# Small loads of the gated delta net issued from GpSimd's queue

## The chip, the cores and the metric

The kernel runs on one core of one Trainium2 chip. The metric is device time in microseconds (us), the median over several executions. Each engine (TensorE or PE, VectorE or DVE, ScalarE or ACT, GpSimd or POOL, SyncE or SP) runs its own instructions in order and waits for the others by semaphores. A DMA is issued by an instruction in the queue of one engine, here SP, ACT or POOL, and an issuing instruction that must wait holds back what stands behind it in that queue. The data then moves on 16 DMA engines that all queues share.

## The reference

A decoder of two layers on 272 tokens (16 learned ones in front of 256) and 2048 channels, in float32. Layer 0 mixes tokens with a short gated convolution, layer 1 with a gated delta net; a gated feed-forward follows each.

```python
def chunked_gated_delta_rule(q, k, v, g, beta):
    ...                                    # chunks of tokens, decay from cumulated g
    t_mat = inverse of (I + strictly lower part of (beta k k^T * decay))
    u_c = t_mat @ (v * beta);  w_c = t_mat @ (k * beta * exp(g))
    for each chunk:                        # the state S goes from chunk to chunk
        v_new = u_i - w_i @ S
        o_i = q_g @ S + (q k^T * decay) @ v_new
        S = S * g_last + k_tail^T @ v_new

def gated_deltanet_mixer(h, ...):          # 16 key heads, 32 value heads of width 128
    qkv, z, b, a = split(h @ w_in)
    ...
    o = rmsnorm(chunked_gated_delta_rule(...), norm_w) * silu(z)
    return o @ w_out
```

## The kernel before

All large products stream their weights. A piece of weights (128 x 1024 float32, 512 KB) is loaded into one of a few `raw` buffers by SP (L95), split exactly into two parts, `whi` by ACT (L108) and `wlo` by DVE or sometimes POOL (L109), and multiplied three times per block by PE (L265 to L267). SP may load a piece only when the split of an earlier one has freed its buffer.

The program order of every engine is fixed: it is the order in which Python emits the instructions (`in_program_order`). `Clockwork` deals this order out in ticks, about one for every 12 large matmuls. `ck.later(n, f)` emits `f` n ticks later, and `ck.side` runs a generator a bit in each tick.

In layer 1 the kernel first computes gates, keys, queries and output gates z. Keys, queries and z go to DRAM (`Kd`, `Qd`, `Zd`), as do the decays `Dd`, the inverses of the diagonal blocks `Ud` (of each 92-token chunk), the blocks `Md`, `Vd` and the factors `Ed`, `Ekd`. Then, between the products with the value weights and the output weights, `cores` runs 16 pairs of value heads. `pair` works as follows.

- It first emits 16 loads, all in one tick: `kh`, `qh` (128 x 276), two each of `D` and `U` (92 x 276, in rows of 92), of `U2`, `M2`, `V2` (46 x 138, in rows of 46) and of the two `e` tiles (128 x 276, one row broadcast to all partitions). `load` (L881) is the helper for D, U, U2, M2 and V2; L894 loads the `e` tiles. The profile names U2, M2, V2 as U, M, V.
- Seven ticks later (`LW`) comes the preparation, in two steps: transposes of kh (L900), products of M2 and U2 (L905), POOL's products of the `e` tiles (L911), products with V2 (L917), POOL's product of U (L922).
- When fewer than two pairs are in their recurrence, the pair starts its own, three chunks of three steps, a step every two ticks. The next pair's loads are emitted one tick after that.
- Two ticks after a pair's last step, `tail` norms its output, `scale` lets POOL multiply (`ot`, L1001) and, right behind that in program order, loads two z tiles (`zl`, L1005). Three ticks later `back` lets DVE form `y` (L1018) from the z tile, and ACT and DVE split it.

The buffers: D, U and kt have three, the `e` tag six (three pairs), kh, qh and zl two, U2, M2 and V2 one.

Of the kernel before, what the change touches and what calls it, by code (L numbers as in the profile page):

```python
# [15 lines left out]
P = 128  # L16
# [5 lines left out]
class Dims:  # L22
# [23 lines left out]
    def gdn_order(self):  # L46
        """the units of the gated delta net: gates, keys, output gates, queries, values, output products"""
        seq = [("ba", 0)] + [("k", j) for j in range(self.NK)] + [("q", j) for j in range(self.NK)]
        seq += [("z", j) for j in range(self.ZE)]
        v = [("v", j) for j in range(self.NV)]  # L50
        z = [("z", j) for j in range(self.ZE, self.NV)]
        for s in range(self.NST):
            seq += v[:self.VA[s]]
            v = v[self.VA[s]:]
            n = len(z) if s == self.NST - 1 else 0
            seq += z[:n]
            z = z[n:]
            seq += [("o", s * self.KT + j) for j in range(self.KT)]
        return seq


class Stream:
    """Weights: DMA, exact split into two float32r parts, some pieces ahead of the products."""

# [11 lines left out]
    def widen(self, pool, raw_bufs, part_bufs):  # L76
        """more buffers for the pieces a0 .. a1 - 1"""
        self.xpool, self.XR, self.XP = pool, raw_bufs, part_bufs
# [48 lines left out]
class Clockwork:  # L127
    """Program order: what runs beside the products is put between their pieces."""

# [46 lines left out]
def trunk(ctx: ExitStack, tc: tile.TileContext, d: Dims, xT, par, w_s0, w_sc, w_sco, w_q, w_k, w_v, w_z, w_ba,  # L176
# [10 lines left out]

# [1 line left out]
    cp = ctx.enter_context(tc.tile_pool(name="const", bufs=1))  # L189
# [17 lines left out]

# [1 line left out]
    def pieces(nk):  # L209
# [25 lines left out]

    # the first products go block by block of channels, as these arrive
    for g in range(KT // G4):
# [42 lines left out]

# [1 line left out]
    hq = [cp.tile([P, G4, T], F32, name=f"h{g}") for g in range(KT // G4)]  # L282
# [15 lines left out]
    def rsqrt_steps(pool, out, v, np_, w, ty, tt, bufs=1):  # L298
        """out = v ** -0.5 : estimate from the exponent, then three Newton steps."""
        y = pool.tile([np_, w], F32, tag=ty, name="rsy", bufs=bufs)  # L300
        t = pool.tile([np_, w], F32, tag=tt, name="rst", bufs=bufs)
        nc.vector.tensor_scalar(out=t.bitcast(I32), in0=v.bitcast(I32), scalar1=1, scalar2=None,
                                op0=ALU.logical_shift_right)
        nc.vector.tensor_scalar(out=y.bitcast(I32), in0=t.bitcast(I32), scalar1=-1, scalar2=0x5F3759DF,
                                op0=ALU.mult, op1=ALU.add)
        for it in range(3):
            nc.vector.tensor_tensor(out=t, in0=y, in1=y, op=ALU.mult)
            nc.vector.scalar_tensor_tensor(out=t, in0=v, scalar=-0.5, in1=t, op0=ALU.mult, op1=ALU.mult)
            nc.vector.scalar_tensor_tensor(out=(out if it == 2 else y), in0=t, scalar=1.5, in1=y,
                                           op0=ALU.add, op1=ALU.mult)  # L310
            yield

    class Norm:
        """x = h * w, split; the per-token factor Rt joins where products leave PSUM."""

# [31 lines left out]
        def finish_last(self):  # L347
            """a token in each partition, then back to a token in each column"""
            a, nt = self.a, (T - self.a) // P
            ps = psum(nt)  # L350
            for i in range(nt):
                for s in (self.acc, self.sq):
                    nc.tensor.matmul(ps[:, i:i + 1], s[:, a + i * P:a + (i + 1) * P], ones[:, 0:1],
                                     start=s is self.acc, stop=s is self.sq)
            v = tp.tile([P, nt], F32, tag="lv", name="lv", bufs=1)
            nc.vector.tensor_scalar(out=v, in0=ps, scalar1=1.0 / d.D, scalar2=EPS, op0=ALU.mult, op1=ALU.add)
            r = tp.tile([P, nt], F32, tag="lr", name="lr", bufs=1)
            for _ in rsqrt_steps(tp, r, v, P, nt, "ly", "lt"):
                pass
            pt = psum(nt * P)  # L360
            for i in range(nt):
                nc.tensor.transpose(pt[:, i * P:(i + 1) * P], r[:, i:i + 1].to_broadcast([P, P]), ident)
            nc.scalar.copy(out=Rt[:, a:T], in_=pt)
# [24 lines left out]

# [1 line left out]
    pctx = more_psum()  # L390
# [31 lines left out]
    with tc.tile_pool(name="scy", bufs=1) as yp, tc.tile_pool(name="sct", bufs=2) as sp:  # L422
# [47 lines left out]
        def resid(nrm, ps, j, a, mode, lag=0):  # L470
            """h += product; what the next norm needs of it, lag units later"""
            nc.vector.tensor_tensor(out=h[j][:, a:T], in0=ps, in1=h[j][:, a:T], op=ALU.add)  # L472
# [30 lines left out]

# [1 line left out]
    def ffn(seq, a, nxt, last):  # L505
# [35 lines left out]

# [1 line left out]
    # a value head 2 j + e of the reference has the row e NK + j here  # L543
    def dram(name, shape):
# [26 lines left out]
    def conv_in(ps, pool, ci, a=0):  # L571
        """causal convolution of width 4 of a unit of the projection, from token a"""
        x1 = pool.tile([P, T], F32, tag="cx", name="cx")
# [17 lines left out]
    st.widen(pha.enter_context(tc.tile_pool(name="wx", bufs=1)), d.XR, d.XP)  # L591
    # a matrix and room to step from its first to its second diagonal block
    W2 = 2 * (H * C + H)
# [73 lines left out]

    # keys, queries
    onehot = ka.tile([P, 2 * NK - 1], F32, name="onehot")
# [15 lines left out]

    # outputs are asked for from token M0 on: queries before it stay zero
    QA = M0 - 4
# [34 lines left out]
    def q_norm(qs):  # L722
        """1 / length of the queries of each token, a column for each chunk of a head"""
        v = small("qv", NK, T)
# [17 lines left out]
    def k_norm(Wt):  # L742
        """1 / length of the keys from the diagonals of their products"""
        for _ in range(d.IL):
# [60 lines left out]
    def inverse(Wt, ri):  # L805
        """unit triangular matrices, one in each partition: the inverses of both diagonal blocks. The heads' own
        preparation joins them to the inverse of the whole; Md takes the block between them, Vd the first inverse,
        both transposed"""
        flat = Wt[:, :CC]
# [50 lines left out]

    # values, recurrence, output
    vts = {}
# [5 lines left out]
    def pair(j, vp):  # L868
        """two heads that share their keys"""
        kh = vp.tile([P, TP], F32, tag="kh", name="kh")  # L870
        nc.sync.dma_start(out=kh, in_=Kd[j])
        qh = vp.tile([P, TP], F32, tag="qh", name="qh")
        nc.sync.dma_start(out=qh, in_=Qd[j])
        JN = slice(j * N, (j + 1) * N)

        def load(tag, src, a, b, bufs, r=slice(None), c=slice(None)):
            """a block of a matrix of each chunk of both heads"""
            t = vp.tile([a, 2, N, b], F32, tag=tag, name=tag, bufs=bufs)
            for e in range(2):
                g = e * NK + j  # L880
                nc.sync.dma_start(out=t[:, e], in_=src[g * N:(g + 1) * N].rearrange(  # L881
                    "n (s c) -> s n c", c=(C if src.shape[1] == CC else H))[r, :, c])
# [7 lines left out]
        for x, xd in ((qg, Ed), (kg, Ekd)):  # L890
            t = vp.tile([P, 2, TP], F32, tag="e", name="e", bufs=6)
            for e in range(2):
                g = e * NK + j
                nc.sync.dma_start(out=t[:, e], in_=xd[g:g + 1, :].broadcast_to([P, TP]))  # L894
            x.append(t)
# [91 lines left out]
        def tail():  # L987
            """norm over the value channels, gate"""
            v = ov.rearrange("c e n -> c (e n)")
# [7 lines left out]
        def scale(steps, ro):  # L997
# [5 lines left out]
            for e in range(2):  # L1003
                z.append(vp.tile([P, S], F32, tag="zl", name="zl", bufs=2))
                nc.sync.dma_start(out=z[e], in_=Zd[2 * j + e])  # L1005
            ck.later(3, lambda: back(0))
# [18 lines left out]
    def cores(vp):  # L1025
        """the recurrences: one pair of heads loads and prepares while others run, a step at a time"""
        wait, core, nxt, started = [], [], 0, 0
# [89 lines left out]

# [1 line left out]
    for k in range(KT):  # L1119
# [9 lines left out]
def in_program_order(tc):  # L1129
    """each engine runs its instructions in the order in which they stand above"""  # L1130
    last = {}
# [9 lines left out]
def layout(d, x, meta_tokens, mixer_norm, ffn_norm, sc_w_in, sc_conv_w, sc_w_out, gdn_w_in, gdn_conv_w, gdn_a_log,  # L1141
# [12 lines left out]

    # the products with the first two groups of columns: block of channels, pair of products, row, ...
    first = np.stack([units(sc_w_in[0][:, g * D:g * D + 2 * P]) for g in range(3)], axis=1)
# [59 lines left out]
```

## Time and profile before

| | |
|---|---|
| time, median of 3 runs | 3058.52 us (3055.4 to 3060.13) |
| profiled execution, first to last instruction (span) | 3051.3 us |
| PE busy | 2910.4 us (95%) |
| DVE, ACT, POOL busy | 61%, 42%, 15% |
| DMA bytes | 539.52 MB, 177 GB/s on average |

The times of the runs lie 4 to 9 us above the span of the profiled execution, which holds only what lies between the first and the last instruction. Busy shares are means over all stages. The pairs of heads run between about 1682 and 2202 us.

### The profile page before, as it was taken

To read this page: it belongs to the slowest core of one execution; us is meant where nothing else is said; L and a number is where in the kernel's file an instruction comes from. 1 tells how busy PE (TensorE), PEld (TensorE's weight loads), DVE (VectorE), ACT (ScalarE), POOL (GpSimd) and SP (SyncE) were. 2 spreads that over 40 slices of the span, in tenths; PEclk is the share of its full clock that TensorE was granted. 3 is DMA by queue.
4 is the path that set the end of the run, shared out by engine and by line. 5 is a ranking of instruction groups with operands and counts; after the bars stand their busy time and mean duration, and the time that the engine had idled before them with its cause. 6 is when DMAs were issued, how large, how long until landed. Compare 5 with 4: busy or idle time off the path is not lost. (4 is left out here: it accounts for less than half of the span.)

```text
span 3051.3 us, 57493 instructions
## 1 busy us (share of the span) xinstructions
PE 2910.4 (95%) x23501; PEld 2875.3 (94%) x23501; DVE 1855.7 (61%) x2570; ACT 1292.7 (42%) x1874; POOL 468.8 (15%) x532
## 2 busy tenths in 40 slices
PE   9999999999999999899988788989899999999998
PEld 8999999999999999888888788888899999999997
DVE  6555555555555456868896466656575555555555
ACT  5334444434334344644333343444354443444434
POOL 2000100000000001524342123322220000000001
PEclk9999999999999999999999889999999999999999
DMA  6555555555555565597556544444555556556565
GB/s 200 191 176 171 178 173 175 176 167 184 178 164 183 168 175 175 166 265 209 184 176 202 155 145 150 147 147 150 160 170 183 184 187 178 196 177 196 184 177 152
DMA packets 212695, 539.52 MB, mean 177 GB/s; under 512 B 55664, under 2 KB 82624, under 8 KB 211952
## 3 DMA queue, kind: packets, MB, share of 16 engines
q1 hardware_dynamic: 208144, 517.92, 54.1%
q0 software_dynamic: 2480, 15.01, 1.7%
q8 instruction: 184, 3.01, 0.4%
q10 hardware_dynamic: 1808, 2.92, 0.3%
q14 instruction: 79, 0.65, 0.1%
HBM read 515.03 MB, written 20.74 MB: 176 GB/s over the span
## 5 line engine op out<-in xcount | busy, mean ns | idle before, releaser
L109 DVE TENSOR_TENSOR wlo<-raw,whi 128x1024 fp32r<-128x1024 f32 (+3 forms) x945 | 1126.0, 1201 | 756.5 <-ACT whi L108 747.7
L267 PE MATMUL mm<-xh,wlo 128*128 128x272 f32 (+2 forms) x5136 | 1479.4, 288 | 34.4 <-POOL wlo L109 22.1
L265 PE MATMUL mm<-xh,whi 128*128 128x272 f32 (+2 forms) x5136 | 1486.7, 289 | 11.9 <-ACT whi L108 11.9
L266 PE MATMUL mm<-xl,whi 128*128 128x272 f32 (+2 forms) x5136 | 1477.0, 288 | 0.5 <-DVE xl L331 0.5
L108 ACT CAST whi<-raw 128x1024 fp32r<-128x1024 f32 (+2 forms) x995 | 962.5, 975 | 542.6 <-PE mm L266 347.1
L267 PEld LDWEIGHTS mm<-xh,wlo 128*128 128x128 f32 x5136 | 978.8, 191 | 41.0 <-POOL wlo L109 26.3
L265 PEld LDWEIGHTS mm<-xh,whi 128*128 128x128 f32 x5136 | 980.1, 191 | 20.6 <-ACT whi L108 12.3
L266 PEld LDWEIGHTS mm<-xl,whi 128*128 128x128 f32 x5136 | 978.0, 190 | 1.2 <-DVE xl L331 1.0
L267 PE MATMUL mm<-ah,wlo 128*128 128x272 f32 (+1 forms) x1408 | 399.3, 284 | 0.0
L265 PE MATMUL mm<-ah,whi 128*128 128x272 f32 (+1 forms) x1408 | 398.9, 283 | 0.0
L266 PE MATMUL mm<-al,whi 128*128 128x272 f32 (+1 forms) x1408 | 398.7, 283 | 0.0
L265 PEld LDWEIGHTS mm<-ah,whi 128*128 128x128 f32 x1408 | 264.9, 188 | 0.0
L267 PEld LDWEIGHTS mm<-ah,wlo 128*128 128x128 f32 x1408 | 264.6, 188 | 0.0
L266 PEld LDWEIGHTS mm<-al,whi 128*128 128x128 f32 x1408 | 264.4, 188 | 0.0
L513 POOL TENSOR_TENSOR u<-u,g 128x272 f32<-128x272 f32 (+1 forms) x88 | 66.5, 755 | 1225.7 <-DVE u L512 1225.7
L580 DVE SCALAR_TENSOR_TENSOR cc<-cx,prm,cc 128x271 f32<-128x271 f32 (+5 forms) x192 | 146.6, 764 | 38.3 <-ACT cc L576 33.3
L109 POOL TENSOR_TENSOR wlo<-raw,whi 128x1024 fp32r<-128x1024 f32 x50 | 131.4, 2627 | 202.1 <-ACT whi L108 163.3
L385 ACT CAST ah<-u 128x272 fp32r<-128x272 f32 (+1 forms) x88 | 36.4, 413 | 289.6 <-POOL u L513 289.6
L343 POOL TENSOR_TENSOR nacc<-nacc,nsq 128x272 f32<-128x272 f32 (+1 forms) x70 | 63.5, 908 | 621.5 <-ACT nsq L341 620.3
L265 PE MATMUL mm<-yh,whi 128*128 128x256 f32 x512 | 152.4, 298 | 0.4 <-DVE h L472 0.4
L266 PE MATMUL mm<-yl,whi 128*128 128x256 f32 x512 | 146.5, 286 | 0.0
L267 PE MATMUL mm<-yh,wlo 128*128 128x256 f32 x512 | 146.4, 286 | 0.0
(327 smaller groups left out, 2316.1 us busy)
## 6 DMA issues: line engine op xcount, KB each, us to landing
raw<-w_gu SPq DMA_DIRECT2D x352, 512.0 KB
raw<-w_dn SPq DMA_DIRECT2D x128, 384.0 KB
raw<-w_sc SPq DMA_DIRECT2D x84, 512.0 KB
raw<-w_dn SPq DMA_DIRECT2D x128, 320.0 KB
raw<-w_z SPq DMA_DIRECT2D x64, 512.0 KB
raw<-w_v SPq DMA_DIRECT2D x64, 512.0 KB
raw<-w_go SPq DMA_DIRECT2D x64, 512.0 KB
raw<-w_sco SPq DMA_DIRECT2D x32, 512.0 KB
```

The source lines that it names most:

```text
L108: self.nc.scalar.copy(out=hi[:, s], in_=t[:, s])
L109: eng.tensor_tensor(out=lo[:, s], in0=t[:, s], in1=hi[:, s].bitcast(F32), op=ALU.subtract)
L265: nc.tensor.matmul(ps, wh, x[0][:, a:b], start=start, stop=False)
L266: nc.tensor.matmul(ps, wh, x[1][:, a:b], start=False, stop=False)
L267: nc.tensor.matmul(ps, wl, x[0][:, a:b], start=False, stop=stop)
L343: nc.gpsimd.tensor_tensor(out=self.acc[:, a:T], in0=self.acc[:, a:T], in1=self.sq[:, a:T], op=ALU.add)
L385: nc.scalar.copy(out=hi, in_=x)
L513: nc.gpsimd.tensor_tensor(out=u1, in0=u1, in1=g1, op=ALU.mult)
L580: nc.vector.scalar_tensor_tensor(out=cv[:, a + i:T], in0=x1[:, a:T - i], scalar=pcol("gcc", 4 * ci + 3 - i), in1=cv[:, a + i:T], op0=ALU.m ...
```

## The change

The DMA instructions of the 16 loads of each pair and of its two z tiles are issued from GpSimd's queue. Each stands in POOL's program order at the place where it stood in SP's. Nothing else is moved; the diff also drops docstrings and comments, which are left out here.

```diff
     def pair(j, vp):
         kh = vp.tile([P, TP], F32, tag="kh", name="kh")
-        nc.sync.dma_start(out=kh, in_=Kd[j])
+        nc.gpsimd.dma_start(out=kh, in_=Kd[j])
         qh = vp.tile([P, TP], F32, tag="qh", name="qh")
-        nc.sync.dma_start(out=qh, in_=Qd[j])
+        nc.gpsimd.dma_start(out=qh, in_=Qd[j])
...
             for e in range(2):
                 g = e * NK + j
-                nc.sync.dma_start(out=t[:, e], in_=src[g * N:(g + 1) * N].rearrange(
+                nc.gpsimd.dma_start(out=t[:, e], in_=src[g * N:(g + 1) * N].rearrange(
...
-                nc.sync.dma_start(out=t[:, e], in_=xd[g:g + 1, :].broadcast_to([P, TP]))
+                nc.gpsimd.dma_start(out=t[:, e], in_=xd[g:g + 1, :].broadcast_to([P, TP]))
...
                 z.append(vp.tile([P, S], F32, tag="zl", name="zl", bufs=2))
-                nc.sync.dma_start(out=z[e], in_=Zd[2 * j + e])
+                nc.gpsimd.dma_start(out=z[e], in_=Zd[2 * j + e])
```

## Rows read from the trace of the kernel before

**Rows 1.** The page: busy time and share of the span, each engine.

```profile
PE 2910.4 (95%) x23501; PEld 2875.3 (94%) x23501; DVE 1855.7 (61%) x2570; ACT 1292.7 (42%) x1874; POOL 468.8 (15%) x532
```

**Rows 2.** Busy time by stretch: length, engines, granted PE clock, DMA share, GB/s.

```profile
1681.60:2201.80 520.20, 454.13 (x3652) 439.15 (x3651) 313.96 (x642) 209.23 (x427) 141.22 (x197) 0.90 0.49 150
1851.00:1863.80 12.80, 12.80 (x111) 12.63 (x110) 7.88 (x23) 4.63 (x9) 3.17 (x3) 1.00 0.38 104
1865.20:1871.70 6.50, 0.92 (x5) 0.29 (x3) 2.00 (x6) 1.21 (x4) 0.00 (x0) 0.82 1.03 303
2300.00:2400.00 100.00, 100.00 (x843) 100.00 (x843) 54.67 (x64) 43.42 (x54) 6.65 (x9) 1.00 0.60 194
```

**Rows 3.** Waits, 1680 to 2250 us: us in total, times, longest.

```profile
POOL sq L980 <- ACT ot L977: 189.7, 26, 14.4
...
ACT whi L108 <- DMA raw<-w_v: 46.2, 8, 13.0
...
DVE y L1018 <- DMA zl<-Zd: 35.7, 7, 9.2
...
PE psd L917 <- ACT Y L908: 32.7, 6, 6.8
...
PE psd L905 <- ACT vn L951: 11.3, 7, 2.0
```

**Rows 4.** SP's queue through one pair's loads: start, length, line, DMA, count.

```profile
1849.73 0.36 SPq L871 DMA_DIRECT2D kh<-Kd  x1
...
1851.74 6.11 SPq L881 DMA_DIRECT2D U<-Ud  x4
1857.89 2.04 SPq L881 DMA_DIRECT2D M<-Md  x2
...
1862.85 0.90 SPq L894 DMA_DIRECT2D e<-Ekd  x2
1863.79 0.91 SPq L1005 DMA_DIRECT2D zl<-Zd  x2
1864.80 14.36 SPq L95 DMA_DIRECT2D raw<-w_v  x5
```

**Rows 5.** Chain of work that ended last: start, length, what.

```profile
1835.32 4.02 DMA zl<-Zd
...
1846.24 0.65 PE psd L917 x12
...
1863.79 4.88 DMA zl<-Zd
...
2036.00 5.78 DMA raw<-w_go
...
2043.77 1.19 PE psd L917 x12
```

**Rows 6.** POOL in order of time: start, length, operation, idle before and releaser.

```profile
1822.73 1.25 POOL L922 TENSOR_TENSOR U<-U,btok 92x276 f32<-92x276 f32 x2 [5.17 <-ACT U L919]
...
1847.89 2.49 POOL L922 TENSOR_TENSOR U<-U,btok 92x276 f32<-92x276 f32 x2
...
2024.30 1.81 POOL L1001 TENSOR_TENSOR ot<-ot,ro 92x384 f32<-92x384 f32 x2 [3.28 <-DVE ro L309]
...
2037.91 1.37 POOL L911 TENSOR_TENSOR e<-e,qh 128x552 f32<-128x552 f32 x1 [2.65 <-PE psd L905]
```

**Rows 7.** Groups of POOL's DMA issues, 1200 to 1690 us: busy us, mean ns.

```profile
L772 POOL DMA_DIRECT2D Wt<-KKd x8 | 4.0, 512 | 6.5 <-DMA KKd<-kk 6.5
...
L759 POOL DMA_DIRECT2D re<-rkd x2 | 1.0, 505 | 0.0
L647 POOL DMA_DIRECT2D glb<-Ld x1 | 0.6, 581 | 0.0
```

**Rows 8.** POOL's DMAs by line: count, KB each, median us from issue to landing.

```profile
glb<-Ld POOLq DMA_DIRECT2D x1, 48.0 KB, 5.1
...
rq<-rqd POOLq DMA_DIRECT2D x1, 17.2 KB, 4.2
```

## The prediction

> **What bounds the kernel now.** The page's first part says PE: busy 95% of the span [rows 1]. That is a mean, so I looked at the stretch in which pairs of heads run, by the view of busy time by stretch [rows 2]. From 1681.6 to 2201.8 us PE is busy 454.1 of 520.2 us at a granted clock of 0.90; from 2300 to 2400 us, where only weights stream, it is busy all the time at 1.00. So 66 us of idle time, and a lower clock around it, are all that this change can win back.
>
> The waits of that stretch [rows 3] show two kinds of stall. In the first, ACT waits for a late piece of weights (46.2 us, 8 times, w_v alone); behind that split in ACT's order stands the copy of `Y`, and PE waits for it before L917: 32.7 us in 6 times. In the second, DVE waits for a z tile before it forms `y` (35.7 us, 7 times); ACT's split of y holds back `vn`, and PE waits at L905 (11.3 us, 7 times) and in what follows. One such stall lies between 1865.2 and 1871.7: PE is busy 0.92 of 6.5 us, at clock 0.82 [rows 2].
>
> What makes both late is SP's queue [rows 4]. The 16 loads of a pair go out from 1849.73 to 1863.75 us, 14.0 us, and no weights in between. The z tiles stand behind them, the weights behind those. Bytes don't set these 14 us: a load of `M` has 24.8 KB and takes 1.02 us, one of `Ekd` 138 KB and takes 0.45. Short rows do: the U loads (rows of 92 and 46 elements) take 6.11 us for four. While they go out, the DMA engines are 38% busy and move 104 GB/s, against 60% and 194 with weights alone [rows 2].
>
> **The change part by part.** It takes 256 loads and 32 z loads out of SP's queue, 14.9 us for each pair, and puts as many instructions on POOL. I treat SP, POOL and the two kinds of stall in turn.
>
> *What 16 loads cost on POOL.* The trace has POOL issues of tiles of 16 rows (`re`), 505 ns, of 48 rows (`Wt`), 512 ns, eight back to back, and of 128 rows (`glb`), 581 ns [rows 7]. None has three runs in a partition. The line through the first and the last is 0.68 ns per run. kh, qh and four e loads have 128 runs (581 ns), four loads of D and U 276 (682), six of U2, M2 and V2 138 (588): 3.5 + 2.7 + 3.5 = 9.7 us. From below: 16 x 0.505 = 8.1 us. From above: what the same 16 cost on SP, 14.0 us, if the thing that paces them there paces POOL. I take 9.7, as it comes from POOL's own rows, and keep both ends. POOL has room: 141 of 520 us busy [rows 2]; 16 x 11 us more makes 61%.
>
> *The stall on the z tile, 7 times.* In these pairs POOL's order is: product of U, the 16 loads, `ot`, the two z loads. By buffers the loads needn't wait: U2, M2 and V2 of the pair before have been read by L905 and L917, which come before the product of U. Before the change, from the end of that product to the landing of the first z tile: 1847.89 + 2.49 = 1850.4 to 1863.79 + 4.88 = 1868.7, 18.3 us; in the shortest pair 1824.0 to 1839.3, 15.4 us [rows 5, 6]. Middle 16.9. After: 9.7 for the loads, 1.8 for `ot` [rows 6], 0.6 for the issue, 5.1 to land, as `glb` needs [rows 8]: 17.2 us. The long path through SP is replaced by one as long through POOL, where `ot`, which SP didn't wait for, is now part of it. 7 x 0.3 = +2 us. Low end 8.1 + 1.8 + 0.5 + 4.2 (`rq`) [rows 8] = 14.6: -16 us. High end 14.0 + 1.8 + 0.6 + 5.1 = 21.5: +32 us.
>
> *The stall on late weights, 6 times.* SP now has nothing ahead of a piece but the wait for its buffer, so it is issued up to 14 us earlier and the 32.7 us go. With them goes some time at the low clock: right after such a stall the twelve L917 take 1.19 us, at full clock 0.65 [rows 5]; with what follows them I count 1 us each time. Together 6 x 6.45 = 39 us. But what is late next is on POOL. In the first two pairs nothing stands ahead of the loads there, and I keep all: 13 us. In the other four, such as the one whose weights land at 2036.00 + 5.78, the loads stand behind `ot`, which waits for DVE until 2024.30 [rows 6]. They start at 2026.1 + 1.2 for the z loads = 2027.3. M2, the ninth and tenth, goes out by 2033.3 and lands at 2038.4, while L905 had finished by 2037.9, when it released POOL's `e` product: 1 us late. The e tiles land at 2027.3 + 9.7 + 5.1 = 2042.1, 4 us late for that product; the product of U stands behind it in POOL's order, and PE needs that for the pair's first step, so I let about half of this come back to PE. I keep 3.3 of 6.45 us, four times: 13 us. Sum -26 us, with ends 0 and -39.
>
> *What queues behind the loads on POOL.* `sq` of the other pair and the e products do; DVE's sum of `sq` waits for it. In the z pairs DVE waits for the z tile later than that anyway; where no stall follows I count nothing, as POOL sits idle 7.3 us on average before `sq` (189.7 us, 26 times) [rows 3] and DVE is busy 314 of 520 us [rows 2]. Without that lead of DVE it costs 9.7 - 7.3 = 2.4 us a pair, at the high end 6.7.
>
> *Rules of the Trainium skill.* The rows say that SP's issue time follows the short rows and not the bytes, with the DMA engines 38% busy [rows 2, 4]. "DMA: Bandwidth & Descriptors" (section "Why a DMA increments its semaphore by 16 and not by 1") says a DMA runs on the largest number of engines, up to 16, that divides the slowest dimension: 4 for 92 partitions, 2 for 46; from SP these are always the lowest-numbered, from GpSimd a cursor moves on from load to load. By that the loads would run beside each other after the change; no run here shows it yet. The same page (section "SWDGE vs HWDGE vs iDMA") speaks against the change: issuing from several engines saves only the issue time, which is usually small beside the transfer. By that nothing would be won; the trace disagrees, as 14.0 us of issue stand against 4.9 us of landing [rows 4, 5].
>
> Sum: +2 - 26 = -24 us. The profiled execution has 3051.3 us of span, the median is 7.2 us above it; -24 makes 3027 of the one and 3034 of the other.
>
> **Rivals.** *POOL is as slow as SP, or slower.* For: the runs of three rows in a partition are on no POOL row, and the U loads cost SP 1.5 us each. Against: POOL's issue hardly grows from 16 to 128 rows. Place: the z pairs, where loads, `ot` and z loads are in a row on POOL. It decides from 26 / 7 = 3.7 us more than before in each of them, that is 13.1 us for 16 loads, 0.82 us each. At 14.0 us, with nothing kept of the late weights since M2 and e land too late, it gives 3058.5 + 32 = 3090; beyond that more.
>
> *The gain is given back.* The weights come early, but in the four later pairs M2, V2 and e come as late as the weights did, and only the first two pairs win, 13 us, while the z pairs lose 7 x 1 to 2 us: 3052 to 3059. For: in the pair at 2027 the e tiles are 4 us late by the sum above. Against: PE doesn't wait for e directly.
>
> *The loads run beside each other.* If what paces them on SP is that few DMA engines serve all of them, and POOL spreads them, they land as fast as POOL issues: the low end in the z pairs and the whole of the weights' term, -16 - 39 = -55, 3003. The first rule of the Trainium skill above is this rival. For: 38% busy engines. Against: the wait of `ot` for DVE and the two-sided price remain.
>
> **How the numbers follow.** Forecast 0.42, spread loads 0.15, given back 0.13, slow POOL 0.30. A measurement of this kernel can tell about 0.2%, 6 us. So faster 0.57, same 0.13, slower 0.30. The time is the forecast's, 3034; its own range is 3015 to 3050. The range of all reaches from the low ends, 3003, to the slow POOL at SP's price, 3090.
>
> **What would show it.** Mean POOL issue of D and U loads 0.6 to 0.7 us: right; over 1.2: wrong, and the sum with it. ACT's wait for w_v and w_go should nearly vanish, and PE's wait at L917 fall below 15 us. DVE's wait for zl should stay near 36 us. If it doubles, POOL is the new bound; if it goes, the loads land faster than I think. PE's granted clock in the stretch should rise from 0.90 to some 0.93.

## The result

The changed kernel takes 3090.31 us (median of 4 runs, 3086.36 to 3092.19), the kernel before on the same chip 3057.57. The ratio is 1.0111, with a 95% interval of 1.0099 to 1.0123: 1.1% slower. The forecast was 3034 us and faster; the time lies 0.3 us past the upper end of the range, at the price of the slow-POOL rival. The profiled execution has 3089.8 us of span, 38.5 more than before. One of the four runs of x12 below took 3963 us at a granted clock of 0.65 and is left out of its row; it is also the run that was traced, so x12 is read by its times alone.

### The profile page after: what moved, and what is told of

It is laid out like the page before. It is cut to its first block, busy times and chain, and to the rows that moved or that the text cites. A ratio compares the mean times of both kernels' runs of the same rounds, so it can differ in the third digit from the quotient of the medians.

```text
span 3089.8 us, 57485 instructions
## 1 busy us (share of the span) xinstructions
PE 2919.9 (95%) x23501; PEld 2881.0 (93%) x23501; DVE 1861.5 (60%) x2570; ACT 1294.6 (42%) x1874; POOL 735.1 (24%) x820
## 5 line engine op out<-in xcount | busy, mean ns | idle before, releaser
L265 PE MATMUL mm<-xh,whi 128*128 128x272 f32 (+2 forms) x5136 | 1489.4, 290 | 10.6 <-ACT whi L108 10.6
L580 DVE SCALAR_TENSOR_TENSOR cc<-cx,prm,cc 128x271 f32<-128x271 f32 (+5 forms) x192 | 144.8, 754 | 37.7 <-ACT cc L576 32.7
```

Source lines behind the costliest of these rows:

```text
L265: nc.tensor.matmul(ps, wh, x[0][:, a:b], start=start, stop=False)
L580: nc.vector.scalar_tensor_tensor(out=cv[:, a + i:T], in0=x1[:, a:T - i], scalar=pcol("gcc", 4 * ci + 3 - i), in1=cv[:, a + i:T], op0=ALU.m ...
```

## The profile after

The page's first part; beside [rows 1], POOL has 288 instructions more and is busy 266 us more, 0.92 us for each.

```profile
PE 2919.9 (95%) x23501; PEld 2881.0 (93%) x23501; DVE 1861.5 (60%) x2570; ACT 1294.6 (42%) x1874; POOL 735.1 (24%) x820
```

Busy time by stretch (columns as in [rows 2]): first the stretch of the pairs with its borders, in the kernel after; then the time in which one pair's 16 loads are issued.

```profile
1640.00:2300.00 660.00, 560.30 (x4433) 541.36 (x4434) 384.88 (x755) 255.16 (x487) 420.39 (x501) 0.90 0.57 148
1864.10:1879.80 15.70, 9.11 (x77) 8.81 (x75) 6.26 (x21) 5.35 (x11) 15.69 (x17) 0.92 0.73 158
```

The same stretch in the kernel before:

```profile
1640.00:2300.00 660.00, 586.75 (x4727) 570.67 (x4726) 411.06 (x811) 276.44 (x530) 167.47 (x226) 0.92 0.50 154
```

PE's idle time in it grows from 73.3 to 99.7 us, by 26.4, and the clock falls from 0.92 to 0.90. PE does 294 matmuls fewer. In the 300 us after it, where weights stream in both kernels, the changed one does 2526; at that rate the 294 are 35 of the 38.5 us. So the loss lies here.

Waits, 1660 to 2300 us, of the kernel after (us in total, times, longest), against [rows 3] (1680 to 2250 us):

```profile
DVE ov L981 <- POOL vt L1105: 67.5, 7, 12.3
DVE ov L981 <- POOL sq L980: 67.3, 12, 12.2
...
PE psc L1016 <- POOL ot L1001: 49.0, 8, 7.5
...
PE psd L905 <- DMA M<-Md: 22.4, 7, 6.6
...
ACT whi L108 <- DMA raw<-w_v: 10.8, 7, 4.2
...
PE psd L905 <- ACT vn L951: 6.5, 2, 5.6
...
PE psd L917 <- ACT Y L908: 4.4, 3, 2.0
...
DVE y L1018 <- DMA zl<-Zd: 3.0, 2, 1.6
```

Both kinds of stall of before are nearly gone: L917 waits 4.4 us and not 32.7, ACT for w_v 10.8 and not 46.2, DVE for the z tile 3.0 and not 35.7. Three others have come in their place. PE waits 49.0 us for `ot` before it transposes it (L1016, in `back`), 22.4 us for M at L905, and DVE 135 us for `sq` or for a small memset that stands behind `sq` in POOL's order (6.2 us before).

POOL in order of time, through one pair's loads, in the kernel after (start, length, what):

```profile
1861.71 2.49 POOL L922 TENSOR_TENSOR U<-U,btok 92x276 f32<-92x276 f32 x2
1864.15 0.59 POOL L871 DMA_DIRECT2D kh<-Kd  x1
1864.73 0.54 POOL L873 DMA_DIRECT2D qh<-Qd  x1
1865.26 2.56 POOL L881 DMA_DIRECT2D D<-Dd  x2
1867.81 4.94 POOL L881 DMA_DIRECT2D U<-Ud  x4
1872.74 2.44 POOL L881 DMA_DIRECT2D M<-Md  x2
1875.17 2.44 POOL L881 DMA_DIRECT2D V<-Vd  x2
1877.60 1.13 POOL L894 DMA_DIRECT2D e<-Ed  x2
1878.72 1.06 POOL L894 DMA_DIRECT2D e<-Ekd  x2
1879.80 1.63 POOL L1001 TENSOR_TENSOR ot<-ot,ro 92x384 f32<-92x384 f32 x2
1881.37 1.12 POOL L1005 DMA_DIRECT2D zl<-Zd  x2
1882.51 0.62 POOL L980 TENSOR_TENSOR sq<-ot 92x256 f32<-92x256 f32 x1
```

The 16 loads take 15.7 us (1864.15 to 1879.80) with no wait among them. `ot`, the z loads and `sq` stand behind them. The two engines that want these, PE and DVE, of the same kernel (in brackets the idle time before and its releaser):

```profile
1880.69 0.72 PE L1016 MATMUL psc<-ident,ot 92*128 92x92 f32 x3 [7.48 <-POOL ot L1001]
```

```profile
1883.16 0.42 DVE L981 TENSOR_REDUCE ov<-sq 92x2 f32<-92x256 f32 x1 [12.22 <-POOL sq L980]
...
1885.30 0.47 DVE L1018 SCALAR_TENSOR_TENSOR y<-psc,prm,zl 128x256 f32<-128x256 f32 x1
```

PE is idle 7.48 us for `ot`, DVE 12.22 us for `sq`. When DVE comes to `y`, the z tile is there.

POOL's groups, 1660 to 2300 us, of the kernel after (count | busy us, mean ns | idle before):

```profile
L881 POOL DMA_DIRECT2D U<-Ud x64 | 78.9, 1238 | 0.0
L881 POOL DMA_DIRECT2D D<-Dd x32 | 41.0, 1284 | 0.0
...
L881 POOL DMA_DIRECT2D M<-Md x32 | 39.0, 1222 | 0.0
...
L1005 POOL DMA_DIRECT2D zl<-Zd x32 | 17.9, 565 | 0.4 <-DMA M<-Md 0.4
...
L871 POOL DMA_DIRECT2D kh<-Kd x16 | 9.3, 582 | 4.2 <-DMA Vd<-wk 4.2
```

The loads of 128 partitions cost what [rows 7] say, 0.54 to 0.58 us. Those of 92 and 46 partitions cost 1.22 to 1.28 us, twice that, whether they have 276 runs (D) or 138 (M).

## The experiments

All ratios are to the kernel before on the same chip; its median was 3051.98 us beside the first four, 3054.09 beside x5 to x8, 3054.98 beside x9 to x12. In kernels with padded rows, line numbers stand 4 to 6 higher.

| kernel | loads on POOL | us | ratio, 95% interval |
|---|---|---|---|
| x2 rows padded | all | 3012.15 | 0.9879 (0.9859 to 0.9900) |
| x3 rows padded | none | 2987.51 | 0.9793 (0.9774 to 0.9811) |
| x4 | all but the ten short-row ones | 3008.83 | 0.9860 (0.9846 to 0.9875) |
| x5 `sq`, `ot` off POOL | all | 3047.48 | 0.9980 (0.9970 to 0.9990) |
| x6 `sq`, `ot` off POOL | none | 3049.03 | 0.9985 (0.9975 to 0.9994) |
| x7 loads two ticks later | all | 3101.82 | 1.0154 (1.0137 to 1.0171) |
| x8 rows padded | all but the ten | 2979.76 | 0.9757 (0.9742 to 0.9772) |
| x9 | z tiles alone | 3037.42 | 0.9941 (0.9922 to 0.9959) |
| x10 padded, `sq`, `ot` off POOL | all | 2983.07 | 0.9762 (0.9748 to 0.9777) |
| x11 padded, `sq`, `ot` off POOL | all but the ten | 2960.57 | 0.9689 (0.9674 to 0.9703) |
| x12 rows padded | z tiles alone | 2989.24 | 0.9789 (0.9771 to 0.9807) |

**What a load costs POOL (x1).** The kernel before, with four loads of each of eight forms from POOL, and as many from SP, behind the last feed-forward. Each form names its partitions, the runs in each and the elements of a run.

```diff
     ffn(seq1, M0, 4, True)
 
+    with tc.tile_pool(name="probe", bufs=1) as pb:
...
+        forms = (("fa", 92, 3, 92), ("fb", 96, 3, 92), ("fc", 92, 1, 276), ("fd", 46, 3, 46), ("fe", 48, 3, 46),
+                 ("ff", 46, 1, 138), ("fg", 128, 3, 92), ("fh", 128, 1, 276))
+        for eng, x in ((nc.gpsimd, "p"), (nc.sync, "s")):
+            for nm_, a, n, c in forms:
...
+                    eng.dma_start(out=t, in_=src)
```

> The kernel before, with eight forms of loads appended after the last feed-forward, four of each back to back, first from POOL, then from SP: fa 92 partitions x 3 runs of 92, fb 96 x 3 x 92, fc 92 x 1 x 276, fd 46 x 3 x 46, fe 48 x 3 x 46, ff 46 x 1 x 138, fg 128 x 3 x 92, fh 128 x 1 x 276. What the POOL issue costs is in dispute; in the changed kernel D, U, M and V cost 1.22 to 1.28 us there, kh, qh and e 0.53 to 0.59. Theory A, the number of partitions (no multiple of 16): fa, fc, fd, ff cost about 1.2 us on POOL, fb, fe, fg, fh 0.5 to 0.6. Theory B, three runs in a partition: fa, fb, fd, fe, fg cost 1.2, fc, ff, fh 0.5 to 0.6. Theory C, the count of runs, which the prediction used: fa and fb 0.7, fd and fe 0.6, fg 0.75. On SP, theory A has fa at 1.3 and fd at 1.0 us once several are queued, and fb, fe, fg near fh's 0.4.

POOL in order of time, in that kernel; the second letter behind "pf" is the one of four, the first the form (a is "fa" above):

```profile
3035.07 1.27 POOL L1127 DMA_DIRECT2D pfab<-w_q  x1
...
3040.15 0.67 POOL L1127 DMA_DIRECT2D pfbc<-w_q  x1
...
3043.93 0.52 POOL L1127 DMA_DIRECT2D pfcc<-w_q  x1
...
3048.53 1.22 POOL L1127 DMA_DIRECT2D pfdc<-w_q  x1
...
3052.12 0.58 POOL L1127 DMA_DIRECT2D pfec<-w_q  x1
...
3053.26 0.55 POOL L1127 DMA_DIRECT2D pffa<-w_q  x1
...
3058.15 0.75 POOL L1127 DMA_DIRECT2D pfgc<-w_q  x1
```

92 partitions with three runs cost 1.27 us, 96 with three 0.67, 92 with one run 0.52; 46 with three 1.22, 48 with three 0.58, 46 with one 0.55. So neither the number of partitions nor the three runs alone doubles the price: both together do. Nor does another engine hold POOL up: while the four loads of 46 partitions go out, from 3046.03 to 3050.97 us, PE, DVE and ACT are not busy at all, as in the cheap loads of 48 partitions behind them. For 96 and 128 partitions the line of the prediction holds (288 runs 0.67, 384 runs 0.75 us). Both queues ran at the same time, so SP's rows are mixed and settle nothing.

**Rows padded to 96 and 48, on either queue (x2, x3).** The DRAM copies get 96 and 48 rows, the loads bring 96 and 48 partitions, the kernel computes with the first 92 and 46. x2 does this to the changed kernel, x3 to the one before.

```diff
-    Dd, Ud = dram("Dd", [NI, CC]), dram("Ud", [NI, CC])
-    Md, Vd = dram("Md", [NI, H * H]), dram("Vd", [NI, H * H])
+    Dd, Ud = dram("Dd", [NI, 96 * C]), dram("Ud", [NI, 96 * C])
+    Md, Vd = dram("Md", [NI, 48 * H]), dram("Vd", [NI, 48 * H])
...
-            t = vp.tile([a, 2, N, b], F32, tag=tag, name=tag, bufs=bufs)
+            q = -(-a // 16) * 16
+            r = slice(r.start or 0, (r.start or 0) + q)
+            t = vp.tile([q, 2, N, b], F32, tag=tag, name=tag, bufs=bufs)
```

> The changed kernel with D, U, U2, M2 and V2 stored in DRAM with rows padded to 96 and 48 and loaded as tiles of 96 and 48 partitions; the products use the first 92 and 46 as before. Four small stores fill the padding once. If the number of partitions sets the price on POOL (theory A), the 16 loads of a pair go from 15.7 to about 9 us, sq and ot are no longer late, and the time comes down from 3090 to what was forecast, about 3034 (3015 to 3050). If the three runs do (theory B), 16 loads stay at 15.7 us and the time at 3090.

> The kernel before (all loads on SP) with the same padded rows. If SP's 14.0 us for 16 loads came from too few DMA engines for 92 and 46 partitions, they fall to about 7 us, z tiles and weights come 7 us earlier, and the time falls by 20 to 60 us, to 3000 to 3040. If the runs set the price on SP, nothing moves: 14 us, 3058.

Both came out below what was expected, at 3012 and 2987 us. POOL in order of time, in x2:

```profile
1864.03 1.38 POOL L887 DMA_DIRECT2D D<-Dd  x2
1865.40 2.47 POOL L887 DMA_DIRECT2D U<-Ud  x4
1867.86 1.15 POOL L887 DMA_DIRECT2D M<-Md  x2
1868.99 1.15 POOL L887 DMA_DIRECT2D V<-Vd  x2
```

SP in order of time, in x3, and then the busy time of the stretch in which its 16 loads are issued:

```profile
1832.07 1.95 SPq L887 DMA_DIRECT2D U<-Ud  x4
1834.14 0.88 SPq L887 DMA_DIRECT2D M<-Md  x2
...
1838.88 0.91 SPq L1011 DMA_DIRECT2D zl<-Zd  x2
```

```profile
1830.00:1838.90 8.90, 8.90 (x77) 8.81 (x76) 7.22 (x25) 4.46 (x10) 3.91 (x5) 1.00 0.77 175
```

On POOL the ten short-row loads fall from 12.4 to 6.2 us, and the changed kernel gets 2.3% faster by the ratios (1.0111 to 0.9879), some 70 us. On SP four U loads take 1.95 us and not 6.11 [rows 4]; 16 loads go out in 8.9 us, not 14.0, with the DMA engines 77% busy, not 38% [rows 2]. So the 14 us on SP weren't the price of short rows as such, as the prediction had it: the rows are as short as before. They came with the count of 92 and 46 partitions. By the Trainium skill's rule in "DMA: Bandwidth & Descriptors" (section "Why a DMA increments its semaphore by 16 and not by 1") a load of 96 or 48 rows is on 16 DMA engines where one of 92 is on 4 and one of 46 on 2. The doubled share agrees with it; which engines a load used was not read. With padding, having no load on POOL (x3) is 25 us better than having all there (x2).

**What stands behind the loads (x5, x6).** x5 takes the two kinds of work that wait behind the loads off POOL, x6 does the same to the kernel before, as a control.

```diff
-            nc.gpsimd.tensor_tensor(out=sq, in0=ot[:, :, n], in1=ot[:, :, n], op=ALU.mult)
+            nc.scalar.activation(out=sq, in_=ot[:, :, n], func=AF.Square)
...
-                nc.gpsimd.tensor_tensor(out=ot[:, e], in0=ot[:, e],
+                nc.vector.tensor_tensor(out=ot[:, e], in0=ot[:, e],
```

> The changed kernel with the two consumers that stand behind the loads on POOL moved off it: sq as a Square on ACT, the product of ot on DVE. The loads keep their price there, 15.7 us for 16. If what cost 33 us is that sq and ot stand behind the loads (DVE waited 135 us for sq and a memset behind it, PE 49 us for ot), the time falls below that of before, to 3010 to 3045, though the z loads still stand behind the 16. If late landing of the loads from POOL is the cost (PE waited 22 us for M), it stays at 3075 to 3090.

> The control for the run above: the same two moves in the kernel before, with all loads on SP. POOL is nearly idle there, so little should come of it: 3040 to 3065. Only the difference between this and its partner is the price of the loads once nothing on POOL waits behind them.

x5 took 3047.48 us, just above its range and by the ratios some 40 us less than the changed kernel; the control moved by 5. So the loss of the changed kernel comes through `sq` and `ot`; x5 moves both at once and does not part them. With them off POOL the move of the loads is worth nothing (0.9980 against 0.9985). Waits, 1650 to 2250 us, in x5:

```profile
DVE y L1018 <- DMA zl<-Zd: 54.0, 7, 8.9
...
PE psc L900 <- DVE y L1018: 29.3, 7, 5.5
...
PE psd L905 <- ACT vn L951: 16.1, 7, 2.6
...
PE psd L905 <- DMA M<-Md: 12.9, 9, 4.5
```

The same in x6:

```profile
DVE y L1018 <- DMA zl<-Zd: 43.9, 8, 10.7
...
PE psd L917 <- ACT Y L908: 32.1, 6, 7.1
```

The wait for the z tile, which the changed kernel had lost, is back and longer than in the control: it had been covered by the wait for `sq`. What the weights give (PE at L917 1.7 us and not 32.1) goes to `y` (29.3 us of PE's waits, 13.9 in x6) and to M (12.9 against 3.9).

**The loads behind `ot` (x7).** The changed kernel, with the next pair's loads emitted two ticks later, behind `ot` and the z loads, and the preparation's lead shortened by as much, so that it stays where it was.

```diff
-            if not wait and nxt < NK and 2 * nxt + 1 in vts and state.get("qdone"):
+            if not wait and nxt < NK and 2 * nxt + 1 in vts and state.get("qdone") and ck.t >= hold:
...
-                wait.append([g, ck.t + d.LW, 0])
+                wait.append([g, ck.t + d.LW - (2 if nxt else 0), 0])
...
+                    hold = ck.t + 3
```

> The changed kernel with the loads of the next pair emitted two ticks later, so that ot, the z loads and the sq beside them come ahead of the 16 loads in POOL's order, and the preparation five ticks after them in place of seven. Order theory (what stands behind the loads pays): PE's wait for ot (49 us) goes, the time falls by 20 to 40 us to 3050 to 3070, with the sq of the next steps late instead. Price theory without order (POOL is simply taken up for 15.7 us wherever the loads stand): about 3090 or more, as the tiles then land late for L905.

It took 3101.82 us: what the theory of the price expected, and not the 3050 to 3070 of the theory of the order. Waits, 1650 to 2250 us, in x7:

```profile
PE psd L905 <- DMA M<-Md: 104.1, 23, 10.4
DVE ov L981 <- POOL sq L980: 97.9, 27, 11.2
```

The wait for `ot` is gone, and PE waits 104.1 us for M. This other place in POOL's order only exchanges one wait for the other; with 15.7 us of issue there was no room for both. DVE still waits 97.9 us for `sq`, while PE's waits for DVE come to 2.0 us in all.

**Which loads to move (x4, x8, x9, x12).** x4 is the changed kernel with L881 back on `nc.sync`, x8 the same on padded rows; x9 is the kernel before with L1005 alone on `nc.gpsimd`, x12 the same on padded rows.

```diff
-                nc.gpsimd.dma_start(out=t[:, e], in_=src[g * N:(g + 1) * N].rearrange(
+                nc.sync.dma_start(out=t[:, e], in_=src[g * N:(g + 1) * N].rearrange(
```

> The changed kernel with the ten loads of D, U, U2, M2 and V2 back on SP; kh, qh, e and z stay on POOL. POOL then issues 8 loads of 0.55 us for a pair, 4.5 us in place of 16.8, SP still 10.6 us. If POOL's price for the ten loads is what cost the 33 us, DVE's waits for sq (135 us) and PE's for ot (49 us) nearly go, and the time falls below that of before, to 3030 to 3050, as the z tile no longer stands behind SP's loads; ACT's waits for weights come back in part (some 30 us). If it were the landing of loads from POOL in general that cost, the time would stay near 3080.

> Padded rows of D, U, U2, M2, V2 on SP (96 and 48 partitions), kh, qh, e and z on POOL. SP's part of a pair should take 5.5 us, POOL's 4.5. If the two gains add (short rows cheap on SP; z tile not behind the loads), the time falls under that of the padded kernel on SP alone, 2987, to 2965 to 2980. If z and e land in time there anyway, it is the same, or some us worse by POOL's order: 2985 to 3000.

> The kernel before with the two z loads alone on POOL, behind ot there; the 16 loads stay on SP. It parts the two stalls of the kernel before. The z tile no longer stands behind 14 us of loads, so DVE's wait for it (36 us, 7 times) should go, the stall on late weights (PE at L917, 33 us, 6 times) stay: 3025 to 3045. If the z tile was only the first of several things late in those pairs, 3050 to 3058.

> Padded rows with all 16 loads on SP and only the z loads on POOL. It says which part of the split pays beside the padding: if it is the z tile, the time is that of the split, 2975 to 2985; if it is kh, qh and e out of SP's way (3.5 us a pair), it stays near 2987.

x4, at 3008.83 us, is better than expected, and by the ratios some 77 us below the changed kernel: having the ten short-row loads on POOL cost more than the whole loss. SP was not relieved by it: its ten loads take 14.4 us in the pair at 1831.88 us and 13.5 to 15.2 in 15 of the 16 pairs, against 10.1 to 11.8 before, when kh, qh and e went out from SP as well. It had been expected to need 10.6. The z tiles alone (x9) win 18 us, inside their range. On padded rows the z tiles add nothing (x12 against x3), while with kh, qh and e they win some 11 us by the ratios, whose intervals just part (x8 against x3).

**Both edits together (x10, x11).** x10 is x2 and x11 is x8, each with `sq` and `ot` moved as in x5.

> All loads on POOL, padded rows (16 loads in 11 us), and sq and ot's product off POOL. If what stands behind the loads on POOL is all that is left of the loss there, DVE's waits for sq (74 us at 3012) go and the time falls to 2985 to 3005. If the z loads, now directly behind the loads, become the next wait as they did with unpadded rows, 3005 to 3020.

> The fastest so far (padded rows on SP, kh, qh, e and z on POOL, 2980) with sq on ACT and ot's product on DVE. DVE waits only some 10 us for sq there, so little is to be had: 2970 to 2985. More than 2990 would say that ACT and DVE pay for the moved work.

x10 came out slightly and x11 clearly below its range. By the ratios x10 is some 36 us below x2. In x2 the ten short-row loads cost POOL the 6.2 us that were forecast for them, and still DVE waited 73.8 us for `sq` or the memset behind it, and PE 9.4 for `ot`. What the two products give with no load on POOL was measured for unpadded rows alone (x6, 5 us). x11, at 2960.57 us, beats both kernels, by 3.1% and 4.2%. Busy time in the stretch of the pairs, in x11:

```profile
1640.00:2300.00 660.00, 646.33 (x5536) 633.96 (x5535) 465.48 (x904) 339.34 (x630) 181.84 (x283) 0.99 0.61 183
```

PE is idle 13.7 us where the kernel before had 73.3, at a clock of 0.99.

## Why the prediction was wrong

**The step that failed: "What 16 loads cost on POOL".** It took 9.7 us, with bounds of 8.1 and 14.0; the trace shows 15.7, above even the high bound. Kh, qh and e were right (3.3 us against 3.5). D and U were taken at 0.68 us and cost 1.28 and 1.24, the small ones at 0.59 and cost 1.22 to 1.24. The line was drawn through rows with one run in a partition [rows 7]; the doubling needs several runs and a partition count such as 92 or 46, and no row had both (x1). The bound of 14.0 was no bound: it took for granted that what paces SP paces POOL by as much. The sentence behind both, that short rows make the 14 us on SP, was wrong too (x3).

**With it fell "What queues behind the loads on POOL".** It was counted at nothing, with the argument that DVE waits for the z tile later than that anyway. But `ot` and `sq` are themselves behind the loads. DVE meets its sum of `sq` before `y`, and PE meets the transposes of `ot` before `y` is formed: 49.0 us of PE in 8 pairs, seven of them those where the z stalls had been. x5 shows that these two together make the loss. By PE's waits it is mostly `ot`: DVE's 135 us reach PE as waits for `h`, `S` and `wlo`, and these grow only from 3.9 to 9.0 us. The 7.3 us by which POOL waits for `sq` on average was read as a cushion, but it is the mean of the 26 `sq` that waited for ACT's `ot`, out of 48; in the pairs where the loads meet `ot` there is none. Nor was the term nothing at the forecast's own price, as x10 against x2 says.

**The stall on the z tile** was expected to stay near 36 us. It is 3.0 us, because DVE is held longer by `sq`, not because the path became short: from the end of the product of U to the landing it is 15.6 + 1.6 + 0.6 + 2.6 = 20.4 us (2.6 being the median landing), against 16.9 before and 17.2 expected. The landing was shorter than the 5.1 us of [rows 8]. Where `sq` is off POOL, the wait is there: 54.0 us in x5.

**The stall on late weights** was right as a mechanism: ACT's wait for w_v falls to 10.8 us, L917 to 4.4 (under 15, as asked), and L905's wait for `vn` from 11.3 to 6.5. What would be late next, M, was named for four pairs at 1 us each. It is late by 3.3 to 6.6 us in just these four (L905 at 2041, 2071, 2176 and 2232 us), 22.4 us in all, since its issue ends 11 us after the first load (1864.15 to 1875.2 in the pair shown), and not 6. (By the prediction's own prices M2 goes out by 2033.5 and not 2033.3, which changes nothing.)

**The sum** by PE's waits needs three rows of the kernel before that [rows 3] leave out:

```profile
PE psc L900 <- DVE y L1018: 9.6, 5, 3.8
...
PE psc L974 <- DVE y L1018: 4.7, 1, 4.7
...
PE psd L905 <- DMA M<-Md: 2.5, 2, 2.2
```

Won are 32.7 - 4.4 = 28.3 us at L917 and 4.8 at L905 for `vn`; lost are 49.0 for `ot` and 22.4 - 2.5 = 19.9 for M, neither of which had a place in the prediction's sum at such a size. That is 35.8 us of loss. Against it stand 14.3 us of PE's waits for `y`, which went with the z stall; some 5 us of small waits came, those for DVE. Together that is 26.4 us, the growth of its idle time. The clock of the stretch, which fell from 0.92 to 0.90 where it was to rise, makes some 12 us, about the rest of the 38.5. That is an estimate: PE's 560 busy us at 0.90 would be 548 at 0.92, and as the two clocks are rounded it may be 6 to 18.

**The rivals.** The slow POOL had the mechanism and a fair price. Its threshold, 0.82 us for a load, was passed: 15.7 / 16 = 0.98. That its 3090 us is the time measured is partly luck: it put the loss on the z tile and kept nothing of the late weights, while in truth the weights were won and `ot`, `sq` and M cost more. Spread loads that land as fast as they are issued are not what the trace shows: M's loads of 24.8 KB take 6.2 us to land, z's of 128 KB 2.6. "The gain is given back" is what is left when `sq` and `ot` are off POOL (x5 against x6), though there it goes to the z tile before it goes to M. The rule of the Trainium skill ("DMA: Bandwidth & Descriptors", section "SWDGE vs HWDGE vs iDMA") that issuing from several engines saves only a usually small issue time was set aside for the 14.0 us that it took SP. That the issue time counted is borne out: the z tiles alone, taken from behind it, won 18 us (x9). But the issue time that the other queue then has is the greater part of this result.

Not settled: why several runs in 92 or 46 partitions cost POOL twice as much. The runs show when it happens, not what POOL does in that time. That padding gave more than expected, in x2 and x3, was not taken apart either; in x2 the loads also land sooner (M after 4.9 us and not 6.2). Nor was it why x11 wins some 21 us over x8, where DVE waited 9.5 us for `sq`, or why SP's ten loads took longer in x4.

## What to carry to other kernels

Before DMAs are moved to a compute engine's queue, price each form by a row of that engine with the same partitions and runs, and ask which of its instructions stands behind them and who waits for it: an engine that is busy 24% of the span can still be late, and in the stretch that counts POOL was busy for 64%. Before a queue is relieved, ask why it is slow: padding 92 and 46 rows to 96 and 48 won 2.1% here without any move (x3). Then move what is cheap to issue, and keep consumers with deadlines off the queue that issues (x11).

## What the runs showed of the hardware

- A load of 92 partitions with three runs each costs POOL 1.25 to 1.31 us, of 96 partitions 0.67, of 92 with one run 0.52 to 0.56; with 46 and 48 partitions it is 1.22 to 1.26 and 0.58 us (x1). The price doesn't follow bytes or runs there.
- On SP the same padding took four U loads from 6.11 to 1.95 us and the DMA engines' share from 0.38 to 0.77 (x3).
- The median z tile of 128 KB lands 2.6 us after its issue from POOL in the changed kernel, 3.3 us in x9 and 4.1 in x4; on SP, behind the pair's loads, it took 4.0 and 4.9 us [rows 5].
- With kh, qh, e and z issued from POOL, SP's ten loads in 92 and 46 partitions took longer, 13.5 to 15.2 us in 15 of 16 pairs and not 10.1 to 11.8 (x4).
